# A third buffer for weights' own values, three for columns on their way to memory, and their halves made every second turn

## The chip, the cores and the metric

The kernel runs on one core of a Trainium2 chip. The metric is the device time of one execution in microseconds; lower is better. The engines of the core work side by side, each through its own queue in order: TensorE (PE, with its weight loads as PEld), VectorE (DVE), ScalarE (ACT), GpSimd (POOL) and SyncE (SP). SP and ACT also issue DMAs here.

## The reference

One step of a hybrid encoder layer, in float32, over 2048 prompt rows and 32 sample rows of width 1024:

```
h = layer_norm(x)                                  # ln_in
z = h @ w_in                                       # 1024 -> 2304, split into three groups of heads
o = concat(A: conv + RG-LRU + GeLU gate,           # a scan over time
           B: retention in chunks + group norm,
           C: sliding-window attention with ALiBi and sinks)
h = layer_norm(alpha * h + o @ w_out)              # ln1
f = (silu(h @ w_gate) * (h @ w_up)) @ w_down       # 1024 -> 2816 -> 1024
h = layer_norm(alpha * h + f)                      # ln2
```

Outputs are h for all rows and the new states of the three groups.

## The kernel before

**Products.** Each float32 product is made of three on TensorE: a matrix is split into a high part (a copy rounded to fp32r) and a low part (what the rounding left), and high·high, low·high and high·low are summed in PSUM. So a unit of weights (128x1024, 512 KB) has to be loaded, copied by ACT to its high part (L250) and subtracted by DVE to its low part (L254) before TensorE can go through it.

**Order of the work.** The prompt is cut into six blocks of rows (256, 384, 384, 384, 384, 256); the 32 sample rows go with block 0. `seq` lists the units in the order in which TensorE takes them: for each block 18 units W of the input projection (`w_unit`, L904) and, one block behind, 8 units O of the output projection (`t_unit`, L991 to L993). Behind them come, for block 0 alone, 44 units G of the gate and up projections (`gu_unit`, L904, 24 matmuls of 288 columns) and 22 units D of the down projection (`t_unit`, twelve matmuls of 512 columns, and eight small ones, L1001, for the sample rows). A group of G is followed by its D: four times 8 G and 4 D, once 4 G and 2 D, and at last 8 G and 4 D; block 5's eight O stand in between. For the rest of the rows (1792) the gate, up and down projections follow in another form (`gu`, L1567, and `down`, L1634 to L1636).

**Weights.** `run` calls, for each unit i, `feed(i)` and `split(i)` twice and then the unit's matmuls. `feed` loads the next units into buffers called `stage` on SP, as long as one of NSTAGE = 2 is free in the order of the program:

```
live = [v for v in staged if not (v < i if raw(v) else v < front["lo"])]
if len(live) >= NSTAGE or (u and known(u - 1) and front["hi"] < u):
    break
```

A unit's buffer is free once its low part is made; of a `raw` unit (O and D of block 0, where the sample rows are multiplied by the weights' own values) only once the unit's matmuls are done. `split` lets ACT make the high parts up to unit i+2 and DVE the low parts up to unit i+1. The pair of parts lies in one of NUNIT = 3 buffers (`pair`). In blocks 1 and 2 the pairs of W and O are also written to memory (`keptW`, `keptO`); later blocks load them from there, without stage, ACT and DVE (L238).

**Side work.** Everything else (the mixers A, B and C of each block, the norms, the transposes) is written as generators. Each unit calls `step()` twice: a turn, which hands out a credit of `rate` and lets the generators advance in rotation until it is spent. The rate is `factor` times the unit's time; `share(SHARE)` sets the factor for blocks 1 to 5 and, up to unit G 14, for the gate and up units. `drain` advances a generator to its end at once.

**Columns.** After a block's ln1, `ln1(b)` stores its rows (L454), waits two turns and runs `to_memory(b)`: each half of a tile of 128 rows is transposed by four small matmuls (L426), copied by ACT into a buffer `stg` (L428) and stored by a DMA that ACT issues (L430 for block 0, L436 for the others). `pipeline(..., 1)` starts a half in each turn of this generator. The columns are read back for the gate and up projections (L467, L1262, L1266, L1308).

Of the kernel before, what the change touches and what calls it, by code (L numbers as in the profile page):

```python
# [9 lines left out]
F32 = mybir.dt.float32  # L10
# [25 lines left out]
GROUPS0 = ((0, 4), (4, 8), (8, 12), (12, 16), (16, 18), (18, 22))  # L36


NUNIT, NSTAGE = 3, 2

FIRST_SHARE, SHARE, LAST_SHARE = 1.4, 1.25, 1.0
GROUPSS = (((0, 3), (3, 6), (6, 9), (9, 12), (12, 15), (15, 17), (17, 19), (19, 22)),) * 2
AFTER = (1, 1)

# [53 lines left out]
def tile_hybrid_step(ctx: ExitStack, tc: tile.TileContext, io, outs):  # L98
# [14 lines left out]
    sb = lefts.enter_context(tc.tile_pool(name="sb", bufs=1))  # L113
# [5 lines left out]
    def sdbank():  # L119
        return ps.tile([128, 512], F32, name="sd", bufs=4)  # L120


    def ptok(b):
        return BLOCKS[b] if b < NBLK else PART
# [4 lines left out]
    def ttiles(b):  # L129
        t = [(i * 128, 128) for i in range(ptok(b) // 128)]  # L130
        return t + ([(ptok(b), DEC)] if b == 0 else [])
# [178 lines left out]
    def pipeline(gens, every):  # L310

        gens, active, n = list(gens), [], 0
        while gens or active:
            if gens and n % every == 0:
                active.append(gens.pop(0))
            cost = 0.0
            for g in active[:]:
                try:
                    c = next(g)
                    cost += 0.5 if c is None else c  # L320
                except StopIteration:
                    active.remove(g)
            n += 1
            yield cost
# [95 lines left out]
    def to_memory(b):  # L420

        def half(t, c0, rows, h):
            p = sdbank().rearrange("p (f c) -> p f c", f=4)
            for f in range(4):
                ft = 4 * h + f
                pe.transpose(p[:, f, :rows], tok[b][t][:rows, ft * 128:(ft + 1) * 128], ident[:rows, :rows])  # L426
            stg = sb.tile([128, 4, 128], F32, name="stg", bufs=5)
            act.activation(stg[:, :, :rows], p[:, :, :rows], AF.Copy)  # L428
            if b == 0:
                act.dma_start(cols0[:, 4 * h:4 * h + 4, c0:c0 + rows], stg[:, :, :rows])  # L430
            else:
                s, off = divmod(START[b] + c0 - START[NBLK], PART)
                for th in range(2):
                    a0, a1 = max(off, th * HALF), min(off + 128, th * HALF + HALF)
                    if a0 < a1:
                        act.dma_start(cols1[s, th, h][:, :, a0 - th * HALF:a1 - th * HALF],  # L436
                                     stg[:, :, a0 - off:a1 - off])
            yield 0.1

        yield from pipeline([half(t, c0, rows, h) for t, (c0, rows) in enumerate(ttiles(b)) for h in range(2)], 1)  # L440

    hA, hOab, hOc, hB = {}, {}, {}, {}

# [7 lines left out]
    def ln1(b):  # L451
        yield from norm(f"m{b}", b, "ln1_g", "ln1_b")
        for t, (_, rows) in enumerate(ttiles(b)):
            sp.dma_start(rows_of(b, t)[:rows, :], tok[b][t][:rows, :])  # L454
        yield from wait(2)
        yield from to_memory(b)
        del tok[b]
        if b + 3 < NBLK:
            load_x(b + 3)
# [1321 lines left out]
    sb = rights.enter_context(tc.tile_pool(name="sb2", bufs=1, side="right"))  # L1781
# [123 lines left out]
```

## Time and profile before

| what | value |
|---|---|
| three timed runs | 2403.1, 2404.89, 2406.81 us; median 2404.89 |
| profiled execution | 2412.02 us, 0.3% above the median |
| its span, first to last instruction | 2410.2 us |
| mean granted TensorE clock | 0.976 of full speed |
| busy: PE, PEld, DVE, ACT, POOL | 95%, 82%, 61%, 33%, 5% |
| DMA | 417.90 MB, mean 173 GB/s |

The window rows shown below give, for a stretch of the span, its length and then for each engine its busy time and the number of its instructions, then the TensorE clock granted, the share of the DMA engines' time and the rate. A row of the waits reads: the engine, tile and line that waited, what ended the wait, and the time in all, the number of waits and the longest. A row of the timeline reads: start, duration, engine, line, operation, tiles, shape, number of equal instructions merged, and in brackets the idle time ahead of it and what ended it; a merged row's duration reaches from its first start to its last end. The chain that ended last explains only the last 44 us here, since it runs from there through 521 us of POOL's own waiting, so the stretches are read instead.

### The profile page before, as it was taken

The numbers are of one execution on the slowest core, as the hardware profiler recorded it, in microseconds if no ns is written. First come the engines' busy times: TensorE is split into PE (matmuls) and PEld (weight loads), VectorE is DVE, ScalarE is ACT, GpSimd is POOL, SyncE is SP. The second block draws the span as 40 slices with busy tenths as digits, with TensorE's granted clock in tenths as the row PEclk, the third lists the DMA queues.
The fourth block names the chain that finished last, engine by engine and source line by source line (L and its number), as shares of the span: only waits on it lengthen the run. The fifth ranks groups of instructions, "written<-read, shape, count | busy, mean of one in ns | idle before, by whom it ended". The sixth has DMA issues, their size and how long they took to land. (4 is left out here: it accounts for less than half of the span.)

```text
span 2410.2 us, 31911 instructions
## 1 busy us (share of the span) xinstructions
PE 2280.2 (95%) x12168; PEld 1969.4 (82%) x12168; DVE 1480.6 (61%) x2656; ACT 789.6 (33%) x1585; POOL 130.8 (5%) x236
## 2 busy tenths in 40 slices
PE   8999999999998988988899999999988999999996
PEld 7887777988888877776779888888877888888884
DVE  7685656556445374357777666767696444544557
ACT  4636255252432333224323223322332212222221
POOL 2010100001001000000000000000000000000003
PEclk9999999999999999989999999999999999999998
DMA  5453485866757754663554334434456433343341
GB/s 195 160 183 123 167 283 185 281 223 237 271 188 285 253 184 149 218 225 118 195 199 142 137 110 162 140 126 156 144 185 214 144 127 109 126 150 118 123 140 61
DMA packets 139272, 417.90 MB, mean 173 GB/s; under 512 B 20272, under 2 KB 35440, under 8 KB 127472
## 3 DMA queue, kind: packets, MB, share of 16 engines
q1 hardware_dynamic: 119056, 407.35, 49.1%
q10 hardware_dynamic: 20064, 8.52, 1.3%
q8 instruction: 96, 1.57, 0.3%
q14 instruction: 56, 0.46, 0.1%
HBM read 316.55 MB, written 99.26 MB: 173 GB/s over the span
## 5 line engine op out<-in xcount | busy, mean ns | idle before, releaser
L1567 PE MATMUL gu<-xh,pair 128*128 128x448 f32 x2464 | 557.4, 368 | 18.8 <-DVE two L1595 7.4
L1567 PEld LDWEIGHTS gu<-xh,pair 128*128 128x128 f32 x2464 | 464.4, 189 | 64.2 <-issue 9.0
L904 PE MATMUL mm<-hAh,pair 128*128 128x384 f32 (+2 forms) x2432 | 433.4, 325 | 26.3 <-DVE pair L254 10.6
L904 PEld LDWEIGHTS mm<-hAh,pair 128*128 128x128 f32 x2432 | 378.0, 192 | 57.9 <-issue 18.3
L1390 ACT ACTIVATE pair<-ww 128x512 fp32r<-128x512 f32 x308 | 189.7, 626 | 519.9 <-PE mm L1636 216.6
L1567 PE MATMUL gu<-xl,pair 128*128 128x448 f32 x1232 | 303.2, 368 | 1.5 <-DVE xl L1319 1.5
L1395 DVE TENSOR_TENSOR pair<-ww,pair 128x512 fp32r<-128x512 f32 x308 | 208.2, 688 | 151.9 <-ACT pair L1390 146.1
L250 ACT ACTIVATE pair<-stage 128x1024 fp32r<-128x1024 f32 x131 | 138.6, 1058 | 356.0 <-DMA stage<-in_wgu 109.0
L1567 PEld LDWEIGHTS gu<-xl,pair 128*128 128x128 f32 x1232 | 232.3, 189 | 22.5 <-DVE xl L1319 2.3
L1634 PE MATMUL mm<-pair,g 128*128 128x512 f32 x571 | 225.1, 394 | 0.1
L1635 PE MATMUL mm<-pair,g 128*128 128x512 f32 x571 | 225.1, 394 | 0.0
L254 DVE TENSOR_TENSOR pair<-stage,pair 128x1024 fp32r<-128x1024 f32 x130 | 159.4, 1227 | 106.1 <-ACT pair L250 105.9
L1636 PE MATMUL mm<-pair,g 128*128 128x512 f32 x571 | 224.6, 393 | 0.0
L1643 DVE TENSOR_TENSOR tok<-tok,mm 128x512 f32<-128x512 f32 x181 | 124.1, 687 | 161.5 <-PE mm L1636 160.4
L904 PE MATMUL mm<-hAl,pair 128*128 128x384 f32 (+2 forms) x1216 | 210.8, 315 | 0.0
L904 PEld LDWEIGHTS mm<-hAl,pair 128*128 128x128 f32 x1216 | 191.9, 192 | 0.3 <-DVE hAl L1129 0.2
L1634 PEld LDWEIGHTS mm<-pair,g 128*128 128x128 f32 x571 | 107.3, 188 | 25.4 <-DVE tok L1641 0.5
L1636 PEld LDWEIGHTS mm<-pair,g 128*128 128x128 f32 x571 | 107.4, 188 | 24.9
L1635 PEld LDWEIGHTS mm<-pair,g 128*128 128x128 f32 x571 | 107.3, 188 | 24.2
L991 PE MATMUL mm<-pair,hCh 128*128 128x512 f32 x216 | 96.1, 445 | 17.3 <-ACT pair L250 11.9
L993 PE MATMUL mm<-pair,hCh 128*128 128x512 f32 x216 | 91.9, 426 | 8.3 <-DVE pair L254 8.2
L992 PE MATMUL mm<-pair,hCl 128*128 128x512 f32 x216 | 90.3, 418 | 0.2 <-DVE hCl L974 0.2
(296 smaller groups left out, 2631.2 us busy)
## 6 DMA issues: line engine op xcount, KB each, us to landing
pair<-keptW SPq DMA_DIRECT2D x63, 1024.0 KB, 5.4
ww<-in_wgu SPq DMA_DIRECT2D x154, 256.0 KB, 3.2
pair<-keptO SPq DMA_DIRECT2D x28, 1024.0 KB, 4.9
stage<-in_win SPq DMA_DIRECT2D x45, 512.0 KB, 4.6
stage<-in_wgu SPq DMA_DIRECT2D x44, 512.0 KB, 3.9
ww<-in_wdn SPq DMA_DIRECT2D x88, 256.0 KB, 3.0
keptW<-pair SPq DMA_DIRECT2D x36, 512.0 KB, 7.3
stage<-in_wdn SPq DMA_DIRECT2D x22, 512.0 KB, 4.3
```

What stands on the lines that cost most here:

```text
L250: act.activation(whi[u], staged[u], AF.Copy)
L254: eng.tensor_tensor(wlo[u], staged[u], whi[u].bitcast(F32), op=ALU.subtract)
L904: pe.matmul(p, w[:, k, :], a[:, k, :], start=(x == 0 and k == 0), stop=(x == 2 and k == 7))
L991: pe.matmul(o, ah[:, cs], wh[:, x, :], start=first and x == 0, stop=False)
L993: pe.matmul(o, ah[:, cs], wl[:, x, :], start=False, stop=last and x == 1)
L1390: act.activation(pairs[key][1], whole_w[x], AF.Copy)
L1395: dve.tensor_tensor(pairs[key][0], whole_w[x], pairs[key][1].bitcast(F32), op=ALU.subtract)
L1567: pe.matmul(bank[n], w[:, k * 128:k * 128 + 128], a[:, k, :], start=first and x == 0 and k == 0, stop=x == 2 and k == 3, skip_group_check= ...
L1634: pe.matmul(bank, gh, wh, start=first and f == fs[0], stop=False)
L1635: pe.matmul(bank, gl, wh, start=False, stop=False)
L1636: pe.matmul(bank, gh, wl, start=False, stop=last and f == fs[-1])
L1643: dve.tensor_tensor(r, r, bank, op=ALU.add)
```

## The change

Four numbers change. There are three buffers `stage` instead of two and three buffers `stg` instead of five (a `stage` takes 4 KB of each partition, a `stg` 2 KB, so the room is the same); `to_memory` starts a half in every second of its turns; and the factor of the credit for blocks 1 to 5 goes from 1.25 to 1.35.

```diff
-NUNIT, NSTAGE = 3, 2
+NUNIT, NSTAGE = 3, 3
 
-FIRST_SHARE, SHARE, LAST_SHARE = 1.4, 1.25, 1.0
+FIRST_SHARE, SHARE, LAST_SHARE = 1.4, 1.35, 1.0
...
-            stg = sb.tile([128, 4, 128], F32, name="stg", bufs=5)
+            stg = sb.tile([128, 4, 128], F32, name="stg", bufs=3)
...
-        yield from pipeline([half(t, c0, rows, h) for t, (c0, rows) in enumerate(ttiles(b)) for h in range(2)], 1)
+        yield from pipeline([half(t, c0, rows, h) for t, (c0, rows) in enumerate(ttiles(b)) for h in range(2)], 2)
```

What this moves is shown at three places. The first is SP's queue at the end of the first eight G units and their four D (`in_wgu` are G's weights, `in_wdn` D's):

```order
 L654 DMA out_p_lru<-lru 128x2
-L245 DMA stage<-in_wgu 128x1024 x2
-L245 DMA stage<-in_wdn 128x1024 x2
+L245 DMA stage<-in_wgu 128x1024
+L245 DMA stage<-in_wdn 128x1024 x3
```

Each load stands one unit further ahead: where two of D's loads were in flight, three are. In the G and D units behind, the rows read alike in both, but each load waits there for the buffer of three units before instead of two.

The second is ACT's queue at the drain of block 5's `ln1`, between units G 13 and G 14 (`stg` are the column buffers, `cols` their place in memory, `pair` the weights of a G unit two further on; in brackets the semaphores that an instruction waits for, of which those named DMAHW are set by landing DMAs). Before:

```order
L428 ACTIVATE stg_9647<-sd_9642 128x512 [waits PE_49]
L436 DMA cols110_90<-stg_9647 512x1x128 [waits Activation_49]
L428 ACTIVATE stg_9655<-sd_9650 128x512 [waits PE_49]
L436 DMA cols111_91<-stg_9655 512x1x128 [waits Activation_49]
L428 ACTIVATE stg_9663<-sd_9658 128x512 [waits PE_49]
L436 DMA cols110_90<-stg_9663 512x1x128 [waits DMAHW6_49,Activation_49]
L428 ACTIVATE stg_9671<-sd_9666 128x512 [waits PE_49]
L436 DMA cols111_91<-stg_9671 512x1x128 [waits Activation_49]
L250 ACTIVATE pair_9683<-stage_9607 128x1024 [waits DMAHW1_49]
```

And now:

```order
L428 ACTIVATE stg_9649<-sd_9644 128x512 [waits PE_49]
L436 DMA cols110_90<-stg_9649 512x1x128 [waits Activation_49]
L428 ACTIVATE stg_9657<-sd_9652 128x512 [waits PE_49]
L436 DMA cols111_91<-stg_9657 512x1x128 [waits Activation_49]
L428 ACTIVATE stg_9665<-sd_9660 128x512 [waits PE_49]
L436 DMA cols110_90<-stg_9665 512x1x128 [waits DMAHW7_49,Activation_49]
L428 ACTIVATE stg_9673<-sd_9668 128x512 [waits DMAHW3_49,PE_49]
L436 DMA cols111_91<-stg_9673 512x1x128 [waits DMAHW1_49,Activation_49]
L250 ACTIVATE pair_9685<-stage_9571 128x1024
```

The fourth copy now waits for a DMA, the store of the first half, because the fourth half takes the first one's buffer; the weights' copy stands behind it in the same place as before.

The third is TensorE's queue in block 2, among the W units (L904, of which hAh x16 and hAl x8 make a unit), where block 0's columns are transposed (L426):

```order
 L426 MATMUL sd<-head,tok 128x128 x4
 L809 MATMUL sd<-kb,zq 128x192 x4
-L904 MATMUL mm<-hAh,pair 128x384 x8
+L904 MATMUL mm<-hAh,pair 128x384 x16
 L904 MATMUL mm<-hAl,pair 128x384 x8
 L426 MATMUL sd<-head,tok 128x128 x4
-L904 MATMUL mm<-hAh,pair 128x384 x8
-L426 MATMUL sd<-head,tok 128x128 x4
-L904 MATMUL mm<-hAh,pair 128x384 x8
-L904 MATMUL mm<-hAl,pair 128x384 x8
-L426 MATMUL sd<-head,tok 128x128 x4
```

Before, a half was transposed in each turn, so two in a unit; now there is one in each unit.

## The prediction

> **What bounds the kernel now.** I read the windows first, cut where the kind of unit changes, since a busy share over the whole span hides the stretches in which TensorE waits. The first three reach to the end of block 5's W and O units, the others cut block 0's G and D.
>
> ```profile
> 0.00:100.00 100.00, 88.50 (x558) 75.12 (x559) 68.09 (x151) 55.60 (x136) 13.87 (x32) 0.95 0.48 162
> 100.00:277.00 177.00, 162.16 (x993) 134.00 (x991) 120.93 (x266) 80.89 (x174) 22.61 (x35) 0.95 0.45 153
> 277.00:853.90 576.90, 561.76 (x3434) 491.48 (x3435) 329.44 (x764) 216.85 (x549) 50.06 (x111) 0.99 0.70 244
> ...
> 853.90:887.60 33.70, 27.58 (x196) 25.77 (x194) 27.36 (x45) 11.19 (x19) 4.44 (x6) 1.00 0.62 203
> 887.60:908.70 21.10, 17.88 (x105) 11.58 (x105) 9.16 (x15) 7.27 (x11) 0.21 (x1) 1.00 0.64 194
> 908.70:937.10 28.40, 27.30 (x193) 25.85 (x194) 16.09 (x24) 11.75 (x17) 0.63 (x3) 1.00 0.58 184
> 937.10:957.50 20.40, 16.48 (x81) 10.07 (x80) 8.38 (x13) 4.56 (x5) 0.21 (x1) 0.92 0.26 81
> 957.50:985.00 27.50, 26.74 (x193) 25.68 (x194) 16.35 (x25) 10.66 (x15) 0.63 (x3) 1.00 0.50 170
> 985.00:1006.10 21.10, 17.70 (x83) 10.52 (x81) 9.46 (x15) 3.51 (x4) 0.21 (x1) 0.84 0.43 150
> 1006.10:1028.30 22.20, 22.20 (x101) 18.12 (x98) 3.89 (x8) 1.67 (x2) 0.00 (x0) 1.00 0.89 331
> 1028.30:1062.80 34.50, 30.14 (x210) 28.79 (x208) 21.07 (x31) 12.22 (x19) 2.96 (x5) 0.95 0.74 248
> 1062.80:1087.10 24.30, 19.35 (x80) 11.84 (x80) 8.60 (x13) 4.90 (x6) 1.07 (x1) 0.79 0.46 170
> ...
> 1103.20:1118.80 15.60, 10.31 (x42) 5.66 (x41) 10.60 (x17) 4.24 (x5) 1.07 (x1) 0.78 0.13 45
> 1118.80:1148.90 30.10, 26.86 (x192) 25.74 (x193) 23.71 (x32) 14.25 (x19) 2.35 (x3) 1.00 0.47 157
> 1148.90:1169.20 20.30, 14.53 (x62) 8.30 (x60) 12.53 (x19) 5.23 (x7) 0.21 (x1) 0.76 0.54 183
> sum 315.30, PE 271.11 PEld 220.97 DVE 179.90 ACT 98.30 POOL 15.07; mean PE 20.85 PEld 17.00 DVE 13.84 ACT 7.56 POOL 1.16
> ```
>
> From 277 to 853.9 TensorE is idle for 15.1 us of 576.9; block 0's G and D leave it idle for 315.3 − 271.1 = 44.2, and the granted clock falls to 0.76 to 0.92 in five of the six D windows. DVE is under 0.9 of every window: no other engine is full. So the waits there, then TensorE's own rows about the end of the second G run:
>
> ```profile
> PE mm L991 <- ACT pair L250: 11.1, 6, 3.0
> PE mm L904 <- DVE pair L254: 8.5, 11, 1.6
> PE mm L904 <- ACT pair L250: 7.9, 9, 1.3
> PE mm L993 <- DVE pair L254: 7.7, 10, 1.2
> PE mm L991 <- ACT hCh L969: 3.3, 1, 3.3
> ```
>
> ```profile
> 933.86 2.29 PE L904 MATMUL mm<-hAh,pair 128*128 128x288 f32 x16
> ...
> 937.06 0.40 PE L991 MATMUL mm<-pair,hCh 128*128 128x512 f32 x1
> ...
> 940.97 0.64 PE L1001 MATMUL mm<-stage,g_s 128*32 128x256 f32 x8
> ...
> 944.55 0.64 PE L1001 MATMUL mm<-stage,g_s 128*32 128x256 f32 x8
> 946.58 0.50 PE L991 MATMUL mm<-pair,hCh 128*128 128x512 f32 x1 [1.40 <-ACT pair L250]
> ...
> 947.85 0.67 PE L993 MATMUL mm<-pair,hCh 128*128 128x512 f32 x1 [0.53 <-DVE pair L254]
> ...
> 949.03 0.63 PE L992 MATMUL mm<-pair,hCl 128*128 128x512 f32 x1
> 949.46 0.63 PE L993 MATMUL mm<-pair,hCh 128*128 128x512 f32 x1
> ```
>
> The first four waits are for a unit's high part (ACT, L250) or low part (DVE, L254): 35.2 of the 44.2. A clean G takes 937.06 − 933.86 = 3.20 us, a clean D 944.55 − 940.97 = 3.58. After two stalls of 1.40 and 0.53 us a matmul lasts 0.63 instead of 0.40 and starts 0.43 behind the last: a stall is paid once as idle time and once more as slow matmuls. Who is late shows in the loads (SP) and ACT's copy:
>
> ```profile
> 941.72 3.86 SPq L245 DMA_DIRECT2D stage<-in_wdn  x2
> 952.78 0.33 SPq L245 DMA_DIRECT2D stage<-in_wgu  x1
> ```
>
> ```profile
> 945.48 1.06 ACT L250 ACTIVATE pair<-stage 128x1024 fp32r<-128x1024 f32 x1 [6.09 <-DMA stage<-in_wdn]
> 946.56 1.23 DVE L254 TENSOR_TENSOR pair<-stage,pair 128x1024 fp32r<-128x1024 f32 x1 [5.89 <-ACT pair L250]
> 947.71 1.28 DVE L1022 TENSOR_TENSOR tok<-tok,mm 128x512 f32<-128x512 f32 x2
> ```
>
> ```profile
> stage<-in_wgu SPq DMA_DIRECT2D x44, 512.0 KB, 3.9
> ```
>
> ACT and DVE had stood idle for 6 us: the load was late. D3's load is issued at 941.72, when D1's matmuls have freed its buffer, its high part is there at 946.54 and TensorE, ready at 945.18, starts at 946.58. One round of a buffer is a load of 3.9, ACT's 1.06, DVE's 1.23 and some 0.4 of issue and hand-over, 6.6 us; over two buffers that is 3.3 per unit against 3.20 of a G. A D holds its buffer to the end of its matmuls, so there both are blocked.
>
> **What a clean stretch would take.** Block 0's 44 G cost 44 × 3.20 = 140.8, 22 D 78.8, block 5's eight O 22.2 (their window is full). The forty transposes of columns add 40 × 0.140 = 5.6, by their weight loads:
>
> ```profile
> L426 PEld LDWEIGHTS sd<-head,tok x40: 137/140/144, 892.6 to 1043.6; 128*128 128x128 f32 x40
> ```
>
> In all 247.4, so 68.0 of the 315.3 are excess: 44.2 idle, the rest mostly slow matmuls. By windows: the first eight G 8.1; the five windows of four D (14.3 each clean) 3.4, since 24 transposes lie in the first of them, then 6.1, 6.8, 10.0 and 6.0, 32.3 in all; the D pair at 1103 8.4; the drain's eight G at 1028 6.7, beside the other transposes; the other four G runs 12.5.
>
> **The third `stage`, in D.** With three, the load of the fourth D goes out when the second D starts, 3.58 earlier than now, and the first G of the next run behind the third D likewise. Issue to high part is 946.54 − 941.72 = 4.8 us (5.3 with half a microsecond for a busy queue) against two D of 7.16: ACT's wait goes. The low part is late next: if DVE does its two accumulations (L1022) first, it is ready 5.3 + 1.28 + 1.23 = 7.8 after the issue, and TensorE wants it behind the D's first two matmuls, at 7.6; so 0.2 to 0.5 remain at some D, with a little slow clock. I return 25 of 32.3, bounds 10 (loads that lengthen) and 32.
>
> **The third `stage`, in G.** 6.6 over three buffers is 2.2 per unit, below 3.20: the load stops setting the pace. What can replace it is NUNIT, and it gives two units (6.4) between a pair's release and its use, of which ACT and DVE take 2.3. Return 9 of 12.5, bounds 3 and 12. The first eight G have DVE at 27.36 of 33.7 with block 5's sums in it, which stay: 3.5 of 8.1, bounds 0 and 7. In the D pair the longest wait, 3.3 us (the fifth row of the waits), is for ACT's hCh, not for weights: 3 of 8.4, bounds 0 and 5. The drain's G keep their 6.7.
>
> **Three `stg`, at the drain.** ACT's rows and the stores:
>
> ```profile
> 1045.67 0.55 ACTq L436 DMA_DIRECT2D cols<-stg  x1
> ...
> 1048.91 0.60 ACT L428 ACTIVATE stg<-sd 128x512 f32<-128x512 f32 x1 [0.74 <-ACT stg L428]
> ```
>
> ```profile
> cols<-stg ACTq DMA_DIRECT2D x28, 256.0 KB, 6.2
> ```
>
> The fourth copy now waits for the store of 1045.67, which lands at about 1051.9 by the median of 6.2, instead of running at 1048.91: 3 us late, 5 where the store takes 8. Behind it in ACT's queue stand its own store and the high part of a G, which TensorE wants one or two units later; its slack of up to a unit (3.2) comes off, the slow matmuls come on. I take −5, bounds −9 and 0 (all of it slack).
>
> **Halves every second turn.** A half waits for nothing new: at one per unit of 384 columns (about 3.20 × 384/288 = 4.3 us) three buffers come round in 12.8, twice the 6.2. It removes crowding that the trace shows once clearly:
>
> ```profile
> 774.15 2.89 PE L809 MATMUL sd<-kb,zq 64*128 64x192 f32 x8 [4.29 <-ACT stg L428]
> ```
>
> There ACT's queue stood at a store's issue until an earlier store had landed, and TensorE 4.29 for the copy behind; with 68.0/44.2 as the factor for slow matmuls that is 6.6 us. I take +6; the bounds are −10 (five passes stall anew, each by half of 4.29) and +13 (a second pass had one like it).
>
> **Loads and credit in blocks 0 and 1.** A third load goes out ahead of tables and small inputs at the start, and W units get the same buffer as G. TensorE idles 11.5 + 14.8 us to 277; I take +6, bounds 0 and 12. From block 3 on the pairs come from memory and pass no `stage`: nothing. SHARE moves side work 8% earlier; in a stretch with 15.1 idle of 576.9 it has little to win or lose: 0, bounds ±5. Behind 1169 all stays in order: 0.
>
> **The sum.** 25 + 9 + 3.5 + 3 − 5 + 6 + 6 = 47.5. The profiled execution took 2412.0, so 2364.5; the median is 7.1 lower, so 2357.4.
>
> **A rule against the trace.** The slow matmuls at 949 follow idle gaps of 1.40 and 0.53 us. The Trainium skill, "TensorE: Matmul & The Clock Gate", section "What's actually happening", has the clock halve after an idle window of about 3.4 us; by it none of these stalls would cost more than itself. That is rival E; the trace so far speaks against it.
>
> **The rivals.**
> - B: DVE or ACT takes the load's place in the G runs. DVE is at 27.36 of 33.7 and 23.71 of 30.1 where sums run beside; if that were the limit, the three terms of G and D pair (15.5) would return nothing: 2373. Against it: at 908.7 and 957.5 DVE is at 0.6.
> - C: three loads in flight lengthen each other. If they take 6 us and more, as the stores do, the high part comes 7 after its issue, the low part 2 us late, and D returns 10: 2372. Against it: DMA is at 0.13 to 0.64 in the D windows. The Trainium skill, "DMA: Bandwidth & Descriptors", section "Issuing engines are not separate DMA queues", says that DMAs from any engine share the same hardware and interleave, which speaks for it; no row of before shows three such loads at once. B and C together give 2357.4 + 15.5 + 15 = 2388.
> - E: stalls cost only themselves, and the slow matmuls come from something that stays. Then the terms of G, D and drain, 35.5, shrink by 44.2/68.0 to 23: 2357.4 + 12.5 = 2370.
> - D: the change doesn't do what it says, because a raw D holds its buffer as before and the third is filled no earlier. 2405, or 2410 with the drain's cost. The order of the loads in the queue speaks against it.
> - A, slower: ACT's queue is blocked in front of column copies. Of 34 halves in six passes 16 come behind a third; if each waits some 7 us (as at 774, 4.29 and the slow matmuls) that is 112: 2357 + 112 = 2469. It decides from about seven such stalls. For it: ACT's queue did stand there before, with five buffers. Against it: the spacing.
>
> **How the numbers follow.** The forecast, with its own range of 2340 to 2366, has 0.58; B 0.10; C 0.10; both 0.04; E 0.02; no effect 0.07; A 0.05; more gain than 17 us beyond it 0.04 (all of the 68.0 in block 0, 2337). From 2337 to 2388 leaves out A, no effect and half of the larger gain. What a measurement of this kernel can tell from no change is about 0.2%, 4.8 us. Faster by more: all but D and A, 0.88; within it 0.07; slower 0.05.
>
> **What the profile after would show.** D loads issued a unit earlier, with PE's wait of L991 for ACT from 11.1 to under 3 us, and a few L993 waits for DVE left; windows of eight G near 27 us and of four D near 16; granted clock 0.95 and more in the D windows. At about 1045 an ACT wait of 3 us for a landing store ahead of the fourth copy. No stall of 4 us by ACT's copy of columns near 774. Wrong would be: ACT rows that wait for `cols<-stg` in every pass (A); loads of 6 us and waits as long as now (C); L904's waits for DVE unchanged (B).

## The result and the profile after

| | median us | ratio to before (95% interval) |
|---|---|---|
| before | 2405.85 | |
| changed | 2332.74 | 0.9697 (0.9678 to 0.9716) |

The kernel is 73 us faster. The forecast was 2357 with a range from 2337 to 2388: the direction was right, the size too small by a third, and the time lies 4 us below the range. The changed kernel's profiled execution took 2332.88 us with a span of 2330.8; that of before, 2412.02, lay 6.2 above the median in this table and above every other run of before on record. So differences between the two traces sum to 79 us, not 73, and a lag of several us against the trace of before may be that execution's own.

The windows of the changed kernel, cut at the same units of TensorE as those of before (length, busy time of PE, PEld, DVE, ACT and POOL, clock, DMA share and rate):

```profile
0.00:96.40 96.40, 88.66 (x587) 76.52 (x588) 68.75 (x153) 59.93 (x141) 13.90 (x32) 0.96 0.55 188
96.40:253.86 157.46, 152.11 (x965) 127.08 (x962) 123.08 (x274) 77.77 (x169) 22.27 (x35) 0.98 0.50 162
253.86:817.49 563.63, 554.85 (x3438) 487.18 (x3435) 326.29 (x756) 217.51 (x548) 61.27 (x111) 0.99 0.72 250
817.49:852.20 34.71, 30.02 (x200) 29.16 (x198) 29.32 (x49) 12.46 (x21) 5.75 (x6) 0.90 0.67 214
852.20:868.00 15.80, 15.80 (x100) 10.91 (x98) 9.86 (x15) 5.12 (x8) 1.15 (x1) 1.00 0.64 201
868.00:894.10 26.10, 26.10 (x200) 26.10 (x198) 14.69 (x22) 13.19 (x19) 3.36 (x3) 1.00 0.67 211
894.10:908.20 14.10, 14.10 (x82) 9.20 (x80) 9.34 (x14) 3.52 (x4) 1.08 (x1) 1.00 0.35 113
908.20:933.90 25.70, 25.70 (x196) 25.67 (x193) 15.38 (x23) 11.76 (x16) 3.23 (x3) 1.00 0.56 184
933.90:948.10 14.20, 14.20 (x83) 9.27 (x81) 8.39 (x13) 2.46 (x3) 1.07 (x1) 1.00 0.55 186
948.10:970.30 22.20, 22.20 (x101) 18.13 (x97) 3.71 (x8) 1.06 (x1) 0.00 (x0) 1.00 0.92 353
970.30:1006.07 35.77, 30.17 (x209) 29.31 (x208) 22.79 (x33) 13.93 (x20) 4.69 (x5) 0.90 0.73 243
1006.07:1020.20 14.13, 14.13 (x82) 9.23 (x80) 8.82 (x13) 3.96 (x5) 1.07 (x1) 1.00 0.76 281
1020.20:1033.10 12.90, 12.90 (x100) 12.88 (x97) 11.62 (x18) 8.21 (x11) 1.07 (x1) 1.00 0.64 205
1033.10:1046.00 12.90, 9.34 (x43) 5.10 (x41) 11.99 (x17) 2.84 (x5) 1.44 (x1) 0.87 0.13 42
1046.00:1071.70 25.70, 25.70 (x197) 25.70 (x194) 22.78 (x31) 14.74 (x20) 3.23 (x3) 1.00 0.56 184
1071.70:1087.70 16.00, 11.59 (x53) 7.69 (x52) 10.98 (x17) 4.24 (x6) 1.07 (x1) 0.89 0.58 198
...
```

In block 0's G and D three windows of four D are 14.1 to 14.2 us, all of it busy at clock 1.00: a clean 14.3 was worked out. The G runs are at 25.7 to 26.1 against a clean 25.6. What is left of idle time stands at three places: the first eight G (34.71), the drain (35.77), and the D pair with the last D. TensorE's waits from 817 to 1088 name them:

```profile
PE mm L904 <- ACT pair L250: 5.1, 1, 5.1
PE mm L991 <- DVE tok L1022: 3.5, 1, 3.5
PE mm L904 <- DVE pair L254: 3.1, 3, 2.0
PE mm L991 <- ACT hCh L969: 2.7, 1, 2.7
...
PE mm L993 <- DVE pair L254: 1.3, 2, 0.9
```

The four waits for weights were 35.2 us and are 9.5, of which one wait of 5.1 is the drain. SP's and ACT's rows at the same D run that the prediction showed:

```profile
886.86 11.16 SPq L245 DMA_DIRECT2D stage<-in_wdn  x3
901.23 3.89 SPq L245 DMA_DIRECT2D stage<-in_wgu  x2
```

```profile
901.45 1.06 ACT L250 ACTIVATE pair<-stage 128x1024 fp32r<-128x1024 f32 x1 [5.29 <-DMA stage<-in_wdn]
```

Three of D's loads are out before the first D ends, the fourth (the last of the x3) at its end, at 897.70; its high part, made at 901.45, is wanted only when the third D ends, at 904.7. ACT waits as long as ever; nobody waits for ACT.

### The profile page after: what moved, and what is told of

Read it like the earlier page. It is cut to its first block, busy times and chain, and to the rows that moved or that the text cites. A ratio compares the mean times of both kernels' runs of the same rounds, so it can differ in the third digit from the quotient of the medians.

```text
span 2330.8 us, 31924 instructions
## 1 busy us (share of the span) xinstructions
PE 2247.1 (96%) x12168; PEld 1959.1 (84%) x12168; DVE 1480.5 (64%) x2656; ACT 790.7 (34%) x1585; POOL 154.9 (7%) x236
## 5 line engine op out<-in xcount | busy, mean ns | idle before, releaser
L904 PE MATMUL mm<-hAh,pair 128*128 128x384 f32 (+2 forms) x2432 | 425.0, 323 | 16.4 <-DVE pair L254 5.8
L904 PEld LDWEIGHTS mm<-hAh,pair 128*128 128x128 f32 x2432 | 376.7, 192 | 41.3 <-issue 17.9
L904 PE MATMUL mm<-hAl,pair 128*128 128x384 f32 (+2 forms) x1216 | 211.9, 317 | 0.0
L904 PEld LDWEIGHTS mm<-hAl,pair 128*128 128x128 f32 x1216 | 193.2, 193 | 0.3 <-DVE hAl L1129 0.2
L254 DVE TENSOR_TENSOR pair<-stage,pair 128x1024 fp32r<-128x1024 f32 x130 | 158.2, 1218 | 32.8 <-ACT pair L250 32.6
L991 PE MATMUL mm<-pair,hCh 128*128 128x512 f32 x216 | 90.3, 418 | 6.1 <-DVE tok L1022 3.5
L993 PE MATMUL mm<-pair,hCh 128*128 128x512 f32 x216 | 86.4, 400 | 1.3 <-DVE pair L254 1.3
```

What stands on the lines that cost most here:

```text
L254: eng.tensor_tensor(wlo[u], staged[u], whi[u].bitcast(F32), op=ALU.subtract)
L904: pe.matmul(p, w[:, k, :], a[:, k, :], start=(x == 0 and k == 0), stop=(x == 2 and k == 7))
L991: pe.matmul(o, ah[:, cs], wh[:, x, :], start=first and x == 0, stop=False)
L993: pe.matmul(o, ah[:, cs], wl[:, x, :], start=False, stop=last and x == 1)
```

## The experiments

Each kernel's ratio is to runs of before taken beside it on the same chip, and ratios are compared.

### Which of the four numbers does it

Four kernels: the changed one with one number set back (`share125`: SHARE 1.25; `stage2`: NSTAGE 2; `every1`: `pipeline(..., 1)`), and before with the buffers alone:

```diff
-NUNIT, NSTAGE = 3, 2
+NUNIT, NSTAGE = 3, 3
-            stg = sb.tile([128, 4, 128], F32, name="stg", bufs=5)
+            stg = sb.tile([128, 4, 128], F32, name="stg", bufs=3)
```

> The changed kernel with the factor of the credit back at 1.25. Before 2405.9, changed 2332.7: 73 us to share out, of which 24 lie before block 2's first unit, 13 in blocks 2 to 5 and 45 in block 0's G and D (less 1.3 later). Theory 1 (the third stage makes the time in blocks 0 and 1 too, the factor is worth about nothing): 2328 to 2338. Rival (the factor makes the larger part of what came off between 100 and 277 us, where it first acts, about 16 us): 2345 to 2352.

> The changed kernel with two stage buffers again; three stg, halves every second turn and 1.35 stay. Theory 1 (third stage: all of 45 in G and D and some 20 of the rest): 2395 to 2402. Rival (factor and spacing make the time outside G and D, 28 us): 2376 to 2384. Above 2406 would say that three stg cost with two stages.

> The changed kernel with a half of the columns in each turn. Theory 1 (the spacing takes away the stall near block 5's part at 774 us and little else): 2338 to 2346. Rival A of the prediction (with three stg and no spacing ACT's queue blocks the copies in every pass): 2350 and more. No use of the spacing: 2329 to 2336.

> The kernel before with three stage and three stg buffers alone (1.25, a half in each turn). Theory 1: 2338 to 2348, the sum of the two kernels above it being about additive. Rival (the three numbers need one another; without spacing three stg stall): 2355 to 2375.

And later, with SHARE = 1.35 alone on before:

> The kernel before with the factor at 1.35 alone. In the four kernels with parts of the change the factor and the spacing together are worth 0.0029, the spacing with 1.35 nothing. Theory (the factor alone takes away the stall of 4.29 us at 774 by another order): ratio 0.996 to 0.999, no such wait at 774. Rival (it needs three stage): 0.999 to 1.003.

| kernel | median us | ratio to before | interval |
|---|---|---|---|
| share125 | 2336.83 | 0.9724 | 0.9709 to 0.9738 |
| stage2 | 2395.60 | 0.9971 | 0.9960 to 0.9983 |
| every1 | 2329.79 | 0.9700 | 0.9686 to 0.9713 |
| buffers_only | 2335.58 | 0.9726 | 0.9713 to 0.9739 |
| share_only | 2393.35 | 0.9947 | 0.9934 to 0.9960 |

The third `stage` with its two `stg` less is worth 0.0274 of before, 66 us. The spacing of the halves is worth nothing: every1 equals the changed kernel, and at 1.25 share125 equals buffers_only. ACT does stand for stores in front of the column copies without it, 16.7 us in seven waits in every1 against 4.9 in one in the changed kernel, but the time does not show it, so rival A falls. The factor is worth 13 us on the kernel before, but with three `stage` only some 6 (0.9726 of buffers_only against 0.9700 of every1; 2 to 11 by their intervals). buffers_only (2335.58 against 2338 to 2348) and share_only (0.9947 against 0.996 to 0.999) both gained more than their theories gave. So the parts do not add up; ACT's waits for loads of in_win to 255 us fell from 49.1 to 32.6 us by the factor alone, which are waits that the third buffer removes too. Where in time, from the starts of the same units in the traces (lag against the profiled execution of before; minus is earlier):

| at | changed | buffers_only | share_only | stage2 |
|---|---|---|---|---|
| block 2's first W (277.6 before) | −23.7 | −25.6 | −7.4 | −4.3 |
| first G (853.9) | −36.4 | −33.9 | −17.7 | −12.9 |
| end of block 0's last D (1173.1) | −80.8 | −80.8 | −21.6 | −16.6 |

These lags carry the slow execution of before: split_load, a kernel further below that takes the time of before (0.9995), starts block 2 at −7.7 and the first G at −13.0. So the clean pair for the third `stage` is stage2 and the changed kernel, which differ in NSTAGE alone: 19.4 lie before block 2's first W, 4.1 from there to the first G, 40.7 in block 0's G and D.

The stall at 774 is gone wherever the order is new, by the factor (share_only, every1) or by the spacing (share125), and stays in buffers_only: from 734 to 814 us before, the stretch gets 5 to 8 us shorter each time. share125 loses as much again between 277 and 387 us, where TensorE waits 6.6 us once for DVE's `tok` (L379), as in none of the others.

### The buffer or the place of the load in the queue

`order2` has three buffers, but `feed` still counts to two. All engines' instructions stand in exactly the order of before; only the waits on buffers differ.

```diff
-NUNIT, NSTAGE = 3, 2
+NUNIT, NSTAGE, ROOM = 3, 2, 3
-                staged[u] = fw.tile([128, 1024], F32, name="stage", bufs=NSTAGE)
+                staged[u] = fw.tile([128, 1024], F32, name="stage", bufs=ROOM)
```

(and three `stg`).

> The kernel before with three stage and three stg buffers, but with feed still counting to two, so that every engine's instructions, SP's loads among them, stand in exactly the order of before; only the waits on buffers change. Against buffers_only (0.9726 of before). Theory (the buffer itself: SP reaches the load early and stands before a buffer that isn't free): ratio 0.972 to 0.978. Rival (the place of the load in SP's queue makes it): 0.985 to 1.0.

2334.60 us, ratio 0.9722 (0.9703 to 0.9740): as buffers_only. It is the buffer that lets the load go; SP had been standing in front of it, up to 277.6 us before for a low part (DVE) or for the end of an O unit's matmuls (PE):

```profile
SPq L245 <- DVE pair L254: 137.0, 31, 9.3
SPq L245 <- PE mm L1001: 48.3, 8, 11.5
```

In order2 these two are 77.6 and 34.2 us.

### Holding or number, in D

`raw_free` keeps two `stage` and lets the sample rows go through the high part of the weights, so that O and D of block 0 no longer hold a buffer to the end of their matmuls; the low part of the sample rows' weights is left out.

```diff
-        return plan[u][0] in "OD" and plan[u][1] == 0
+        return False
...
-                t_unit(b, ("D", half), [G[k] for k in (f0 + 2 * kp, f0 + 2 * kp + 1)], wh, wl, staged.get(i),
+                t_unit(b, ("D", half), [G[k] for k in (f0 + 2 * kp, f0 + 2 * kp + 1)], wh, wl, wh.bitcast(F32),
```

(and the same for O).

> The kernel before with two stage, in which the sample rows are multiplied by the weights' high part instead of their own values (their low part is left out), so that a stage is free once its low part is made in O and D as in W and G. Theory (in the D runs it is the holding to the end of the matmuls that costs, not the number: 6.6 us of a round over two is 3.3 per unit, under 3.58): 25 to 32 us of D come back, some 3 of block 0's O: ratio 0.985 to 0.9885. Rival (two buffers are too few whatever holds them): 10 or less, 0.996 to 1.0.

2361.95 us, ratio 0.9837 (0.9819 to 0.9856), a little more than the theory's upper end. The first four windows of four D took 21.1, 20.5, 21.1 and 24.4 us before, 18.2, 15.1, 15.1 and 17.9 here, 15.8, 14.2, 14.2 and 14.2 in the changed kernel: 20.8 of the 28.7 come from the holding. A second piece was not in the prediction at all: block 0's O, which also hold their buffer, run 10.3 us faster (228 to 277.6 before).

### Blocks 0 and 1: a queue that stands

The prediction gave these 6 us; by the lags 24 came, 26 with the buffers alone, 19 between stage2 and the changed kernel. TensorE's waits there name the weights for 3.7 us in all, so here is one such place of before, followed from TensorE back (PE, DVE, ACT):

```profile
126.15 0.89 PE L733 MATMUL sd<-head,b_o 128*128 128x128 f32 x2 [2.91 <-DVE b_o L727]
```

```profile
123.28 0.42 DVE L687 TENSOR_TENSOR b_k<-sd,tb 128x256 f32<-128x256 f32 x1 [2.99 <-ACT b_v L685]
...
125.41 1.09 DVE L727 TENSOR_SCALAR b_o<-sd,b_mv,b_rs 128x64 f32<-128x64 f32 x4
```

```profile
121.91 1.06 ACT L250 ACTIVATE pair<-stage 128x1024 fp32r<-128x1024 f32 x1 [6.10 <-DMA stage<-in_win]
122.88 0.36 ACT L685 ACTIVATE b_v<-sd 128x256 f32<-128x256 f32 x1
```

ACT stands 6.10 us at the high part of a W unit whose load is late. Behind it in ACT's queue is mixer B's copy `b_v`; DVE waits 2.99 for it, and TensorE 2.91 for what DVE makes next. The wait is called `b_o`; its cause is `stage`. In buffers_only the same stretch has no such wait, and from this W unit's start to the next one's it takes 7.6 us instead of 12.6. ACT's and DVE's waits to 255 us, before, then in buffers_only:

```profile
ACT pair L250 <- DMA stage<-in_win: 49.1, 18, 8.5
ACT pair L250 <- DMA stage<-in_wout: 16.6, 3, 9.3
...
DVE pair L254 <- ACT pair L250: 23.1, 7, 7.8
```

```profile
ACT pair L250 <- DMA stage<-in_wout: 13.3, 4, 4.6
ACT pair L250 <- DMA stage<-in_win: 11.5, 3, 8.1
...
DVE pair L254 <- ACT pair L250: 4.0, 2, 2.2
```

Two experiments tried to spare ACT that wait with two buffers: `pool_high` gives the copies of W and O to POOL, `late_high` puts them later in ACT's queue.

```diff
-        act.activation(whi[u], staged[u], AF.Copy)
+        pool.tensor_copy(whi[u], staged[u]) if plan[u][0] in "WO" else act.activation(whi[u], staged[u], AF.Copy)
```

> The kernel before (two stage, five stg) with the high parts of the W and O units (blocks 0 to 2) copied by POOL instead of ACT. ACT stood 65.7 us in front of such copies waiting for loads in the first 255 us before, 24.8 with three stage alone. Theory (the time in blocks 0 and 1 was lost because ACT's queue stood and the mixers' copies behind it came late): 10 to 20 us of the 26 come back although no load is earlier: ratio 0.9915 to 0.996. Rival (the weights themselves were late): nothing, or worse where POOL's copy is longer than ACT's 1.06: 1.0 to 1.01.

```diff
-        while front["hi"] < min(front["dma"], i + NUNIT):
+        while front["hi"] < min(front["dma"], i + (2 if plan[i][0] in "WO" else NUNIT)):
```

> The kernel before (two stage, five stg) in which ACT makes the high parts of units up to i+1 instead of i+2 during W and O, so that a copy stands later in ACT's queue, behind more of the mixers' copies; TensorE's, DVE's and POOL's instructions keep their order, and only the kept parts' place in SP's queue moves with the numbers. Theory (in blocks 0 and 1 the time is lost because a queue stands at the copy of a load that has not landed and the mixers' work behind it is late; with POOL as that queue DVE's L727 waited 2.60 us for POOL's b_rs as it had for ACT's b_v): 8 to 20 us come back: ratio 0.9915 to 0.9965. Rival (the weights themselves were late, so a later copy costs more): 1.001 to 1.015.

pool_high: 2408.98 us, 1.0024 (1.0012 to 1.0036). My theory's number is missed, the rival's met, but not for the rival's reason alone. POOL's copy has a median of 1.04 us against ACT's 1.06, though single ones last up to 2.02 (ACT's 1.11). POOL's queue now stands instead, for the loads and, nearly as long, for TensorE to give a `pair` back, and the same chain hangs on POOL's part of mixer B. How the loss divides between these is open. POOL to 280 us, then DVE:

```profile
POOL pair L250 <- DMA stage<-in_win: 63.6, 17, 9.6
POOL pair L250 <- PE mm L904: 53.7, 13, 9.2
...
POOL b_rs L723 <- DVE b_rs L721: 6.5, 2, 3.4
```

```profile
128.97 1.10 DVE L727 TENSOR_SCALAR b_o<-sd,b_mv,b_rs 128x64 f32<-128x64 f32 x4 [2.60 <-POOL b_rs L723]
```

late_high: 2389.66 us, 0.9933 (0.9920 to 0.9946), in the theory's range, with TensorE's order untouched. But by the lags only 6.3 of it lie before block 2, no more than in split_load, and the rest by 588 us, so this does not show that the gain is from blocks 0 and 1. To 255 us ACT hardly waits for W's loads any more, and DVE does:

```profile
ACT pair L250 <- DMA stage<-in_wout: 17.1, 4, 7.6
ACT pair L250 <- DMA stage<-in_win: 3.8, 4, 1.5
...
DVE pair L254 <- ACT pair L250: 58.9, 25, 6.5
```

So moving the copy moved the wait to another queue; only the earlier load removed it from ACT and DVE alike. What is followed from end to end is the one place at 126 us; that the rest of the time in blocks 0 and 1 went the same way is argued from the sums of the waits.

Why the loads are late there was tried in two ways: `no_keep` writes no pairs to memory (keeps and known return False), `split_load` loads a unit in two DMAs.

> The kernel before without keptW and keptO: no pair is written to memory, and the later blocks load and split all units through the two stage buffers. Only the part to block 2's first W unit (277.6 us before) is compared, in which TensorE's order is the same; behind it there is more work for ACT and DVE. Theory (in block 1 a load lands 5 to 8.5 us after its issue because stores of pairs run beside it, and that makes ACT's queue stand): block 2 starts 4 to 12 us earlier and ACT's waits for loads of in_win before 255 us fall from 49.1 to under 30. Rival (the round of two buffers is too long without any stores): within 2 us, 45 and more.

> The kernel before with each load of a stage as two DMAs of half the columns. Theory (the length of the load in the round of two buffers costs): if the halves land within 3.2 us, as the 256 KB loads of ww do, the round falls from 6.6 to 5.9 and G runs, D runs and blocks 0 and 1 get 8 to 20 us back: ratio 0.9915 to 0.9965. Rival (the two halves take as long together as the one did): 0.999 to 1.003, and ACT's waits for loads as before.

no_keep, of which there is a single execution: block 2 starts 11.3 us earlier than in the trace of before, at the upper end. The median load of in_win, over the whole span 4.6 us before, is

```profile
stage<-in_win SPq DMA_DIRECT2D x108, 512.0 KB, 3.7
```

but that counts the later blocks' loads too; up to 277 us it falls from 4.3 to 3.7. ACT's wait for it falls to 33.8, short of the 30 expected. The one load of 8.5 us (113.33 to 121.84 before, with two stores of pairs behind it) takes 4.1. The stores beside the loads are thus a part of the cause, but how large a part is open: split_load, next, has 7.7 of these 11.3 us without any gain in time, and no_keep takes the stores out of SP's queue as well as from beside the loads. split_load: 2399.04 us, 0.9995 (0.9982 to 1.0007), the rival's number. Each half lands sooner,

```profile
stage<-in_win SPq DMA_DIRECT2D x90, 256.0 KB, 3.4
```

but two must, and ACT's wait for in_win was 39.2 in the profiled execution; the time does not move. How far a truly shorter load would replace the third buffer stays open.

### The drain

The changed kernel's ACT at the drain, and TensorE behind it:

```profile
995.27 0.60 ACT L428 ACTIVATE stg<-sd 128x512 f32<-128x512 f32 x1 [4.87 <-DMA cols<-stg]
...
996.47 1.06 ACT L250 ACTIVATE pair<-stage 128x1024 fp32r<-128x1024 f32 x1 [0.60 <-ACT stg L428]
```

```profile
997.58 0.85 PE L904 MATMUL mm<-hAh,pair 128*128 128x288 f32 x2 [5.07 <-ACT pair L250]
```

The fourth copy waits for the first one's store, as forecast. `split_first` puts the high part ahead of the four copies; `drain_later` drains after f = 16 instead of 14:

```diff
-    finish(f"m{NBLK - 1}")
+    do(lambda n=sum(s[0] != "do" for s in seq): (feed(n), split(n))); finish(f"m{NBLK - 1}")
```

> The changed kernel with the high part of unit G 15 put ahead of the drain's four copies of columns in ACT's queue instead of behind them. The changed profile has a stall of 5.07 us there and the eight G from 970 to 1006 take 35.8 against 34.5 before. Theory (the high part behind the waiting fourth copy is what TensorE waits for): the eight G take 31 to 32.5, the time 2327 to 2330. Rival (the next high part or the gate's copy behind the same wait comes late instead): 35 to 36, 2331 to 2334.

```diff
-    q_gu(0, 12, 14)
+    q_gu(0, 12, 16)
...
-    q_gu(0, 14, FT)
+    q_gu(0, 16, FT)
```

> The changed kernel with block 5's ln1 drained after four more G units (gate and up units to f = 16 instead of 14), so that its four halves of columns come out one per unit and the fourth finds its stg free. The change of factor and the next part's side work move back with it. In split_first the wait of 4.02 us stayed in ACT's queue and the next low part was 5.22 us late instead. Theory (the wait for the store itself is the cost): no ACT wait over 1 us for cols stores there, the eight G from 970 to 1006 take 29 to 31.5 instead of 35.8, 2326 to 2330. Rival (the side work that comes later takes it back before the last D): the eight G shorter, but 2331 to 2336.

split_first: 2332.99 us, 0.9716 (0.9698 to 0.9735), nothing gained. ACT still waits, and the next unit's low part is late by as much:

```profile
995.83 0.60 ACT L428 ACTIVATE stg<-sd 128x512 f32<-128x512 f32 x1 [4.02 <-DMA cols<-stg]
```

```profile
999.16 2.29 PE L904 MATMUL mm<-hAh,pair 128*128 128x288 f32 x8 [5.22 <-DVE pair L254]
```

drain_later: 2326.35 us, 0.9669 (0.9657 to 0.9682). The four halves come 2.5 to 4.6 us apart, none waits, and the eight G take 30.7:

```profile
970.20:1000.90 30.70, 29.14 (x215) 28.14 (x214) 23.75 (x35) 14.60 (x22) 5.06 (x6) 1.00 0.69 232
```

The wait itself was the cost. The side work that moved back also helped the D pair by 5 us and cost 4 at the last D. By its profile (2323.8 against 2330.8) and its ratio this is the fastest single edit, some 6 us ahead of the changed kernel, though the two intervals overlap a little. With late_high on top (`both`) nothing more came:

> The changed kernel with the high parts made up to i+1 during W and O and the drain four units later, the two edits of late_high and drain_later together, as a candidate that beats the changed kernel. With three stage ACT still stands 24.8 us before loads up to 255 us. Theory (queues that stand): 2318 to 2328. Rival (with three stage the loads are early enough and a later copy only costs): 2330 to 2345.

2327.83 us, 0.9665 (0.9651 to 0.9679): at the upper end of the first theory by time, but its profile shows blocks 0 and 1 11 us slower than the changed kernel (block 2's first W at −12.6 instead of −23.7). That fits the rival, by which a later copy only costs there with three `stage`, but its profiled execution (a span of 2331.3) was the slowest of its five, so it is not shown.

## Why the prediction was wrong in size

By its own terms (profiled executions, us returned):

| term | forecast | bounds | measured |
|---|---|---|---|
| D runs, five windows | 25 | 10 to 32 | 33.0 |
| G runs | 9 | 3 to 12 | 11.6 |
| first eight G | 3.5 | 0 to 7 | −1.0 |
| D pair | 3 | 0 to 5 | 2.8 |
| drain | −5 | −9 to 0 | −1.3 |
| blocks 0 and 1 | 6 | 0 to 12 | 23.7 |
| from 277 to 854 | 6 (column stores), 0 (factor) | −10 to 13, ±5 | 12.7 |
| behind 1169 | 0 | none | −2.1 |

The sum was 47.5 and the traces have 79.4; of the 31.9 missing, blocks 0 and 1 are 17.7, D 8.0, the stretch from 277 to 854 6.7.

- **The step that failed is "Loads and credit in blocks 0 and 1".** Between stage2 and the changed kernel, too, it measures 19.4, above its bound of 12. That bound was made from TensorE's idle time with the weights looked for by name, and I set most of the 26 us aside as waits of mixers. Three things were missed: ACT's 65.7 us in front of loads, which hand their wait to the mixers behind them in the queue; block 0's O, which hold their buffer like D (10.3 in raw_free); and the slow matmuls that follow idle time, which cost there as in D: TensorE's busy time to block 2 fell from 250.7 to 240.8 us for nearly the same instructions.
- **D** was right in its mechanism and mis-sized. I had kept 0.2 to 0.5 us of late low parts at some D, because DVE would do its sums first; in the trace four of the five windows have no idle time at all.
- **277 to 854.** That pairs come from memory "from block 3 on" holds, but block 1's O and half of block 2's W and O still come through `stage`: buffers_only gains 8.5 from 277 to 441. Kernels with two buffers gain there against the same trace too (stage2 5.8, split_load 4.0), so little of it is shown to be the buffer's. The stall at 774 went and its 5 to 8 us with it, but spacing alone is worth nothing in the median (0.9724 against 0.9726), so the +6 came about by luck, through the new order. A factor "worth 0" is worth 13 us on the kernel before.
- **The drain** was read rightly, place and waiter; after 4.87 us of ACT's wait TensorE stood 5.07. The window got 1.3 longer and not 5 since its other G got faster: without the wait it is 30.7.
- **Rivals.** B, DVE as the bound, may hold for the first eight G alone, which did not get shorter and have DVE at 29.32 of 34.71, which no run tested; the G runs behind are clean. C falls: a load of in_wgu took 4.2 us instead of 3.9, and one of in_wdn 3.8 instead of 4.3. D falls. E falls: from the first G to the last D 45 us went (315.3 to 270.2), of which idle time is 26 (44.2 to 18.3); a saved stall returned 1.7 times itself, and of the six D windows five had a clock of 0.76 to 0.92 before, while four have 1.00 now and the two that still wait 0.87 and 0.89. The rule of the Trainium skill ("TensorE: Matmul & The Clock Gate", "What's actually happening"), read so that stalls this short cost no clock, does not hold here: behind stalls of 1.40 and 0.53 us matmuls lasted 0.63 us instead of 0.40. That of the Trainium skill's "DMA: Bandwidth & Descriptors", "Issuing engines are not separate DMA queues", agrees with no_keep: without the stores the loads up to 277 us took 3.7 us instead of 4.3.

## What to carry to other kernels

A load that lands late costs not only who wants its data: any engine that works in order and has the first step on it in its queue stands, and all work behind it is late under other names. So before bounding what an earlier load is worth, sum the waits of the *copying* engine for the load, and follow what stands behind each. Here moving such a step to another engine or later moved the wait (1.0024 and 0.9933 of before); another buffer (0.9726), or a buffer given back earlier (0.9837), removed it.

## What of the hardware was not expected

- POOL's copy of 128x1024 float32 to fp32r had a median of 1.04 us, ACT's 1.06; the longest were 2.02 and 1.11.
- Two loads of 256 KB landed in a median of 3.0 to 3.4 us each where one of 512 KB took 3.9 to 4.6, with no gain in time.
